# The first MLP by seven products of quarters, with its squares through DRAM and the state-space matrices written beside its down half

## The chip, the cores and the metric

One core of one Trainium2 chip runs the whole program. The metric is the device time of one execution in microseconds. The core's engines work side by side, each through its own list of instructions in order: TensorE (PE, with the weight loads PEld beside it), VectorE (DVE), ScalarE (ACT) and GpSimd (POOL). SyncE (SP) issues nearly all DMAs from one queue, in order as well.

## The reference

Two layers on x of 1024 tokens by 1024 channels, all in float32:

```python
for i in range(2):
    u = rms_norm(h, norm_mix[i])
    h = h + (diff_attention(u, ...) if i == 0 else s5_layer(u, ...))
    h = h + square(relu(rms_norm(h, norm_ffn[i]) @ w_up[i])) @ w_down[i]
```

`w_up[i]` is 1024 by 4096 and `w_down[i]` 4096 by 1024. The S5 layer (a state-space layer: a complex diagonal recurrence in both directions over 64 groups of 16 channels, then a gated projection) depends on its parameters through matrices that can be made at any time before it: input and output matrices, rotations and short convolution kernels for every group.

## The kernel before

Activations lie transposed: a tile of 128 channels by 1024 tokens, eight of them in `hT`. A float32 product is made of three: operand and weight are each split into a rounded high part (ACT) and the remainder (DVE), and high x high, low x high and high x low are summed in PSUM (`mm3`, L202). So 128 x 1024 outputs over 1024 channels take 8 x 3 x 2 = 48 matmuls of 512 columns. Weights come through `WStream` in tiles of 512 KB: three raw buffers, ACT makes `whi` (L66), DVE makes `wlo` (L67).

**The stages** in order: q, k and v projections; attention; the output projection `wo` (`psw`); the first MLP; the S5 layer with its gated projection; the second MLP; the transposed write of the output.

**The first MLP** (`run_mlp`) goes in eight blocks of four hidden tiles. `up(f)` makes a hidden tile with 48 matmuls (`psu`), DVE applies relu and the norm (`mz`, L649), ACT squares, ACT and DVE split the square into `sh` and `sl`, which stay in SBUF. `down(b)` multiplies a block's four tiles into all eight tiles of the output (`psd`, 24 matmuls each) and DVE adds each to `hT` (L667). Over the MLP that is 1536 matmuls up and 1536 down.

**The second MLP** has another scheme already. Input and weights of two hidden tiles (a pair, 16 in all) are cut in quarters, and seven products of sums of quarters stand for eight (Strassen's way): a pair takes 7 x 12 = 84 matmuls (`psX`, `psY`, `psQ`, L986) in place of 96. DVE and ACT make the sums and splits of the next pair's weights meanwhile (`w_sums_a`, `w_sums_b`, `w_group_a`, `w_group_b`, L844 to L879), DVE adds up the products and applies relu (`finish`, L996), and the squares go to DRAM (`sD`) and are read back (`sr`) for the down half, which runs in four blocks of eight hidden tiles, 48 matmuls for each of 32 steps. This part stands in a manual schedule: its instructions keep the order in which they are written. Everything else is ordered by the framework's scheduler, which works by a simulated timeline: it hoists an instruction to where it believes that its engine would be free.

**The state-space matrices** are made by `Prep`: `start` computes powers and angles (161 small instructions on DVE), and `tile(kt)`, eight times, makes the matrices of eight groups. A tile's work: products of 128 elements on POOL (B, C), then in four quarters the matrix W (six complex-product instructions of 256 elements on DVE, L1295 to L1297), PE transposes, ACT copies, `INd` to DRAM; the matrix Y (six instructions of 256 elements on POOL, one buffer `Yt`), `Yd` to DRAM; small matmuls (`ppk`); and the rotations R (42 DVE instructions in seven doubling levels, one buffer `Rt`, L1295 to L1297), `Rd` to DRAM. At the end the kernel matrix goes to `Kd`. In this kernel `start` stands ahead of the first MLP and `tile(b)` ahead of `down(b)`. The S5 layer reads all of it back, and starts with transposes of `hT` (`pu`) and, after `pin` and a copy, its scans on DVE (L1506 is the first instruction of one).

Of the kernel before, what the change touches and what calls it, by code (L numbers as in the profile page):

```python
# [104 lines left out]
def _build(ctx, tc, nc, a, out):  # L105
# [41 lines left out]
    def mlp_src(i):  # L147
        r = []
        for b in range(9):
            ups = [(kt_cols(wup[i], f * P, P), (8, P)) for f in range(4 * b, 4 * b + 4)] if b < 8 else []  # L150
            dns = (
                [
                    (wdn[i][(b - 1) * 512 : b * 512, q * 256 : (q + 1) * 256].rearrange("(k p) n -> p k n", p=P), (4, 256))
                    for q in range(4)
                ]
                if b
                else []
            )
            r += ups[:1] + dns + ups[1:]
        return r  # L160
# [22 lines left out]
    for f in range(32):  # L183
        src.append((kt_cols(wup[1], f * P, P), (8, P)))
    for b in range(4):
        for m in range(KT):
            src.append((wdn[1][b * 1024 : (b + 1) * 1024, m * P : (m + 1) * P].rearrange("(k p) n -> p k n", p=P), (8, P)))
# [345 lines left out]
    hT = hv.tile([P, KT, S], F32, name="hT", tag="hv")  # L533
    prep = Prep(const, tc, nc, a, dram, ident)
    ctx.callback(prep.close)
    mlp = phase.enter_context(tc.tile_pool(name="mlp", bufs=2, reuse_waits="tile"))
    psm = phase.enter_context(tc.tile_pool(name="psm", bufs=2, space=PSUM, reuse_waits="tile"))
    turn = [0]

    def acc_tile(name):  # L540

        if psl is None:
            return psm.tile([P, S], F32, name=name, tag="ps")
        turn[0] += 1
        if turn[0] % 3:
            return psm.tile([P, S], F32, name=name, tag="ps")
        return [psl.tile([P, 512], F32, name=name, tag="b") for _ in range(2)]

    def pieces(ps):

        if isinstance(ps, list):
            return [(slice(512 * t, 512 * t + 512), ps[t]) for t in range(2)]
        return [(slice(0, S), ps)]

    def bank(ps, t):
        return ps[t] if isinstance(ps, list) else ps[:, 512 * t : 512 * t + 512]

    class Norm:
# [16 lines left out]
        def done(self):  # L575
# [5 lines left out]
            for c, b in pieces(ps):  # L581
                nc.scalar.activation(self.acc[:, c], b, AF.Ln, bias=eps_t, scale=1.0 / D)
# [196 lines left out]

    xs = {}
# [833 lines left out]
```

## Time and profile before

| what | value |
|---|---|
| median of 3 runs | 2500.45 us (2498.51 to 2503.64) |
| the profiled execution | 2497.23 us, its span 2495.3 us |
| granted TensorE clock, mean | 0.994 |
| busy: PE / DVE / ACT / POOL | 97% / 66% / 41% / 12% |
| chain that ended last | PE 71%, DVE 18%, ACT 3%, DMA 3%, issue 3% |

Busy shares are means over stages of quite different kinds. The chain of waits is followed back from the last instruction, at each step to what released it. Matmuls follow each other at a shorter distance than the duration shown for one, since they are pipelined: the distance is read from the chain, where a piece has a count and a length. In the stretches of the view by windows, busy time counts overlapping instructions once.

### The profile page before, as it was taken

The page shows a single profiled execution, that of the slowest core. Times are in us where ns is not written, and L with a number is a line of the kernel's source. Part 1 is how long each engine was busy: PE and PEld are TensorE (multiplying, and loading weights), DVE is VectorE, ACT ScalarE, POOL GpSimd, SP SyncE. Part 2 cuts the span into 40 slices and gives each one's busy share as a digit, 9 for nine tenths or more (in the row PEclk, how much of TensorE's full clock was granted, in tenths as well). Part 3 has the DMA queues.
Part 4 walks back from the last instruction along what each step waited for, and adds up shares of the span by engine and source line. Part 5 has one row for each costly group of instructions (what it writes and reads, how often), then busy time and mean ns, then how long its engine had stood idle before and what let it go on. Part 6 is the DMA issues. An engine that isn't in the chain of part 4 may idle for free.

```text
span 2495.3 us, 33696 instructions
## 1 busy us (share of the span) xinstructions
PE 2409.3 (97%) x12338; PEld 2031.0 (81%) x12338; DVE 1635.3 (66%) x3473; ACT 1019.1 (41%) x1808; POOL 299.6 (12%) x452
## 2 busy tenths in 40 slices
PE   7999999999998999999999997999999999999999
PEld 6889988888787778778788886787878888788887
DVE  5765188888468898888873457994876666432321
ACT  5654277777242212222122137883454333321111
POOL 1221000000004242242241230000000000000000
PEclk9999999999999999999999998999999999999999
DMA  6666524231212232322232236552223334632322
GB/s 158 187 182 181 118 64 102 56 97 43 61 43 77 82 95 78 95 86 84 87 94 65 70 136 184 171 164 76 85 70 112 103 110 135 198 110 68 101 59 60
DMA packets 295173, 258.78 MB, mean 104 GB/s; under 512 B 43232, under 2 KB 266080, under 8 KB 295008
## 3 DMA queue, kind: packets, MB, share of 16 engines
q1 hardware_dynamic: 289120, 248.00, 33.9%
q10 hardware_dynamic: 5888, 8.63, 1.3%
q8 instruction: 97, 1.59, 0.3%
q14 instruction: 68, 0.56, 0.1%
HBM read 180.09 MB, written 68.09 MB: 99 GB/s over the span
## 4 chain that ended last, share of the span: by engine, by line
PE 71%; DVE 18%; ACT 3%; DMA 3%; issue 3%; SPq 1%; POOL 0%; ACTq 0%; DVEq 0%; POOLq 0%
PE psd L202 22%; PE psu L202 9%; PE psq L202 7%; PE psX L986 6%; PE psw L202 4%; PE pss L425 3%; PE po L475 3%; PE psh L216 3%; PE psQ L986 3%; DVE tr L1296 2%; DVE Rt L1297 2%; PE pT L462 2%; PE psg L202 2%; DVE wlo L67 1%; DVE mx L432 1%
## 5 line engine op out<-in xcount | busy, mean ns | idle before, releaser
L66 ACT ACTIVATE whi<-wraw 128x1024 fp32r<-128x1024 f32 (+1 forms) x145 | 152.7, 1054 | 618.3 <-PE psd L202 298.3
L202 PE MATMUL psd<-sh,wlo 128*128 128x512 f32 x1024 | 329.1, 397 | 0.0
L202 PE MATMUL psd<-sh,whi 128*128 128x512 f32 x1024 | 324.7, 395 | 0.0
L202 PE MATMUL psd<-sl,whi 128*128 128x512 f32 x1024 | 323.3, 394 | 0.0
L67 DVE TENSOR_TENSOR wlo<-wraw,whi 128x1024 fp32r<-128x1024 f32 (+1 forms) x145 | 178.7, 1233 | 86.7 <-ACT whi L66 86.6
L202 PEld LDWEIGHTS psd<-sl,whi 128*128 128x128 f32 x1024 | 191.0, 188 | 40.2
L202 PEld LDWEIGHTS psd<-sh,wlo 128*128 128x128 f32 x1024 | 191.2, 188 | 39.7
L202 PEld LDWEIGHTS psd<-sh,whi 128*128 128x128 f32 x1024 | 190.2, 188 | 38.5
L1127 DVE TENSOR_TENSOR hT<-hT,psd 128x512 f32<-128x512 f32 x64 | 41.2, 684 | 206.0 <-PE psd L202 206.0
L432 DVE TENSOR_REDUCE mx<-pss 128x1 f32<-128x1024 f32 x128 | 155.4, 1221 | 13.8 <-PE pss L425 13.8
L440 ACT ACTIVATE e<-pss,mx 128x1024 f32<-128x1024 f32 x128 | 142.9, 1116 | 52.2 <-DVE mx L432 49.6
L202 PE MATMUL psu<-ah_u,whi 128*128 128x512 f32 x512 | 159.5, 392 | 0.0
L202 PE MATMUL psu<-ah_u,wlo 128*128 128x512 f32 x512 | 158.6, 391 | 0.0
L202 PE MATMUL psu<-al_u,whi 128*128 128x512 f32 x512 | 158.4, 391 | 0.0
L475 PEld LDWEIGHTS po<-V,pt 128*128 128x128 f32 x1024 | 128.0, 191 | 5.5
L475 PE MATMUL po<-V,pt 128*128 128x128 f32 x1024 | 132.4, 275 | 0.0
L202 PEld LDWEIGHTS psu<-ah_u,whi 128*128 128x128 f32 x512 | 95.6, 188 | 21.0 <-issue 0.7
L202 PEld LDWEIGHTS psu<-al_u,whi 128*128 128x128 f32 x512 | 95.7, 188 | 19.7
L202 PEld LDWEIGHTS psu<-ah_u,wlo 128*128 128x128 f32 x512 | 95.7, 188 | 19.6
L845 DVE TENSOR_TENSOR wlo<-wraw,whi 128x1024 fp32r<-128x1024 f32 x48 | 58.8, 1226 | 75.9 <-ACT whi L844 75.9
L667 DVE TENSOR_TENSOR hT<-hT,psd 128x512 f32<-128x512 f32 (+1 forms) x88 | 80.3, 922 | 40.6 <-PE psd L202 40.6
L1297 DVE TENSOR_TENSOR Rt<-Rt,tr 128x2 f32<-128x2 f32 (+6 forms) x448 | 102.2, 228 | 6.3
(401 smaller groups left out, 5342.6 us busy)
## 6 DMA issues: line engine op xcount, KB each, us to landing
wraw<-in_ffn_w_up_dram SPq DMA_DIRECT2D x64, 512.0 KB, 4.4
wraw<-in_ffn_w_down_dram SPq DMA_DIRECT2D x64, 512.0 KB, 3.7
sr<-sD SPq DMA_DIRECT2D x32, 512.0 KB, 4.3
wraw<-in_attn_w_qkv_dram SPq DMA_DIRECT2D x24, 512.0 KB, 4.8
sD<-s SPq DMA_DIRECT2D x48, 256.0 KB, 2.2
xt<-in_x_dram SPq DMA_DIRECT2D x16, 512.0 KB, 5.8
zs<-z ACTq DMA_DIRECT2D x64, 128.0 KB, 4.4
q<-qs SPq DMA_DIRECT2D x16, 512.0 KB, 6.7
```

Of the source, the lines that this page charges most:

```text
L66: self.nc.scalar.activation(hi, t, AF.Copy)
L67: self.nc.vector.tensor_tensor(lo, t, f32(hi), op=ALU.subtract)
L202: nc.tensor.matmul(ps[t] if isinstance(ps, list) else ps[:, c], wt[:, k, n0 : n0 + P], x[k][:, c], start=k == 0 and i == 0, stop=k == nk - ...
L216: nc.tensor.matmul(ps, wt[:, kk, n0 : n0 + P], x[k][:, c], start=start and kk == 0 and i == 0, stop=stop and kk == last and i == 2)
L425: nc.tensor.matmul(ps[:, c], q[:, qt * P : (qt + 1) * P], k[:, c], start=i == 0, stop=i == 1)
L432: nc.vector.tensor_reduce(mx, w["ps"][m], axis=AX.X, op=ALU.min)
L440: nc.scalar.activation(e, w["ps"][m], AF.Exp, bias=w["mx"][m], scale=-1.0, accum_out=s)
L475: nc.tensor.matmul(w["po"], w["pt"][:, k, :], V[:, k, h * P : (h + 1) * P], start=k == 0, stop=k == KT - 1)
L667: nc.vector.tensor_tensor(hT[:, m, c], hT[:, m, c], p, op=ALU.add)
L845: nc.vector.tensor_tensor(lo, raw, f32(hi), op=ALU.subtract)
L986: nc.tensor.matmul(ps, wt[:, j, kk, :], xx, start=start and kk == 0 and i == 0, stop=kk == 3 and i == 2, skip_group_check=not start)
L1297: E.tensor_tensor(o, o, tmp, op=op)
```

## The change

The scheme of the second MLP becomes a function, `fast_up(lay, tail, ...)`, with the down half in `down(u, on_step, on_last)`, and the first MLP uses both. `TailO` gives what runs at the head of the manual schedule: in layer 0 the last three tiles of the output projection, as the last two of the gated projection in layer 1. The first MLP's PSUM tiles are six banks of 512 in place of eight, since two are kept for `Prep`. SBUF has no room for all of it at once, so `hT` goes to DRAM (`hA`) tile by tile, comes back into another tile, `hTb`, once the operands B11 and R1 are used up, and its old place becomes the memory of `Prep` (`prepmem`, cut up by `Carve`). After the down half `hT` is read back once more (`hTc`) into the place of `prepmem`. `Prep.start` is written behind the up half, and `tile` once in four steps of the down half, the eighth behind the last step. R is made for four groups at a time, in half as many instructions of twice the size.

```diff
     def mlp_src(i):
-        r = []
-        for b in range(9):
...
+        r = [(kt_cols(wup[i], f * P, P), (8, P)) for f in range(32)]
+        for b in range(4):
+            for m in range(KT):
+                r.append((wdn[i][b * 1024 : (b + 1) * 1024, m * P : (m + 1) * P].rearrange("(k p) n -> p k n", p=P), (8, P)))
         return r
...
+    def fast_up(lay, tail, gp, xpool, wx, gw, nacc, open_banks, free_ops, first_f):
...
-    def run_mlp(i, hi, lo, on_last, on_block):
...
+    def down(u, on_step, on_last):
+        bank1, hid, nf, ring = u["bank1"], u["hid"], u["nf"], u["ring"]
+        while nf < 8:
+            u["split"](nf)
+            nf += 1
+        for b in range(4):
+            for m in range(KT):
+                w = ws.next()
...
+                    mm3(ps, w, 0, ([y[0] for y in x], [y[1] for y in x]), halves=halves)
+                for t in range(2):
+                    c = slice(512 * t, 512 * t + 512)
+                    nc.vector.tensor_tensor(hT[:, m, c], hT[:, m, c], ps[t], op=ALU.add)
...
+                on_step(b, m)
+                if b == 3:
+                    on_last(m)
...
+    st = phase.enter_context(tc.tile_pool(name="st0", bufs=6, space=PSUM, reuse_waits="tile"))
+    psl = phase.enter_context(tc.tile_pool(name="psl0", bufs=2, space=PSUM, reuse_waits="tile"))
...
+        nc.sync.dma_start(h0[m], hT[:, m, :])
...
+    up0 = fast_up(0, TailO(), gp, {"B11": xpa, "R1": xpa, "B21": xpb}, wx, gw, nacc, banks0, ("B11", "R1"), 1)
+    xpa_stack.close()
+    hT = pool("hB").tile([P, KT, S], F32, name="hTb")
+    for m in range(KT):
+        nc.sync.dma_start(hT[:, m, :], h0[m])
+    prep = Prep(const, tc, nc, a, dram, ident, hv.tile([P, KT * S], F32, name="prepmem", tag="hv"))
+    prep.start(psl)
...
+    down(up0, lambda b, m: prep.tile(2 * b + m // 4) if m % 4 == 3 else None, last0)
...
+    hT = hv.tile([P, KT, S], F32, name="hTc", tag="hv")
+    for m in range(KT):
+        nc.sync.dma_start(hT[:, m, :], hD[m])
...
-            R = t("Rt", (2, 2, P))
+            if hf % 2 == 0:
+                continue
+            q4 = slice(g0 + 2 * hf - 2, g0 + 2 * hf + 2)
+            R = t("Rt", (4, 2, P))
```

**DVE in the up half of the first MLP.** Before, between two hidden tiles (`mz` is a hidden tile's relu, `Rt` and `tr` the rotations):

```order
L1297 TENSOR_TENSOR Rt<-Rt,tr 128x2x32
L1296 TENSOR_TENSOR tr<-Rt,sn 128x128
L649 SCALAR_TENSOR_TENSOR mz<-psu,nacc 128x512
L1297 TENSOR_TENSOR Rt<-Rt,tr 128x2x64
L649 SCALAR_TENSOR_TENSOR mz<-psu,nacc 128x512
L67 TENSOR_TENSOR wlo<-wraw,whi 128x1024
L1296 TENSOR_TENSOR tr<-Rt,cs 128x128
```

In the changed kernel, in the fourth pair (`wraw` lines are the next pair's sums of quarters, `s_7425` a sum of products, `prepmem` is what `Prep` makes: 128x4 and 128x4x2 are levels of R, 128x8x2x16 parts of W):

```order
L621 SCALAR_TENSOR_TENSOR wraw<-wraw 128x512
L1350 TENSOR_TENSOR prepmem<-prepmem 128x4
L622 TENSOR_TENSOR wraw<-wraw 128x512
L1349 TENSOR_TENSOR prepmem<-prepmem 128x4
L1348 TENSOR_TENSOR prepmem<-prepmem 128x4x2 x2
L795 TENSOR_TENSOR s_7425<-s_7425,psX 128x512
L1348 TENSOR_TENSOR prepmem<-prepmem 128x8x2x16 x2
L1350 TENSOR_TENSOR prepmem<-prepmem 128x4
L722 SCALAR_TENSOR_TENSOR s_7425<-s_7425,nacc_6121 128x512
L1350 TENSOR_TENSOR prepmem<-prepmem 128x8x2x16
L1349 TENSOR_TENSOR prepmem<-prepmem 128x4x2
```

The scheduler has moved the work of `Prep` from where it is written, behind the up half, into the up half: between the first pair's products and the first addition of the down half DVE has 864 of its instructions (163 of `start`, 571 of R, 115 of W, 15 others), and 194 stand beside the down half (133 of R, 55 of W, 6 others); 25 follow it.

**SP between the up and the down half.** `sr` are the squares that come back for the down half (the first step takes the hidden tiles 0 to 7), `hTb` waits for the last use of R1, in the sixteenth pair:

```order
L739 DMA sr<-sD_2_6889 128x1024
L1001 DMA hTb<-hA_6143 128x1024
L1001 DMA hTb<-hA_6144 128x1024
L1001 DMA hTb<-hA_6145 128x1024
L1001 DMA hTb<-hA_6146 128x1024
L739 DMA sr<-sD_3_6890 128x1024
L1001 DMA hTb<-hA_6147 128x1024
L1001 DMA hTb<-hA_6148 128x1024
L1001 DMA hTb<-hA_6149 128x1024
L1001 DMA hTb<-hA_6150 128x1024
L739 DMA sr<-sD_4_6891 128x1024
```

Before, no such load stood between the first MLP's halves, and its squares did not go through DRAM.

**PE at the end of the first MLP.** Before (`psd` down half, `pp` and `kk` the last of the eighth tile of `Prep`, `psr` the norm of the tokens, `pu` the first of the S5 layer):

```order
L202 MATMUL psd<-sh,wlo 128x512 x2
L1415 MATMUL pp_14024<-ident,kk 128x128
L1415 MATMUL pp_14027<-ident,kk 128x128
L590 MATMUL psr<-ones,nacc 128x1 x8
L1439 MATMUL pu<-ident,hT 128x128 x8
```

In the changed kernel (`ppc` opens a tile of `Prep` on PE):

```order
L190 MATMUL psd<-sh,wlo 128x512
L889 MATMUL psr<-ones,nacc_9325 128x1
L1430 MATMUL pp_12809<-ident,prepmem 128x128
```

and from the last `psr` on:

```order
L889 MATMUL psr<-ones,nacc_9325 128x1 x4
L1473 MATMUL pp_12877<-ident,prepmem 128x128
L1473 MATMUL pp_12880<-ident,prepmem 128x128
L1374 MATMUL ppc<-ident,prepmem 128x128 x2
L1392 MATMUL pp_13173<-prepmem 128x128
L1393 MATMUL pp_13173<-prepmem 128x128
L1430 MATMUL pp_13190<-ident,prepmem 128x128 x2
```

The eighth tile of `Prep` has moved from beside the down half to behind it: all of its rows on PE, from `ppc` on, stand between the last `psd` and `pu<-ident,hTc`, which comes 17 rows below the last one shown. On POOL the two clears of the S5 layer's `X` now stand ahead of that tile's C and Y products, and on SP the eight loads of `hTc` stand behind its last store.

## Rows read from the trace of the kernel before

**Rows 1.** The page's busy times: us, share of the span, instructions.
```profile
PE 2409.3 (97%) x12338; PEld 2031.0 (81%) x12338; DVE 1635.3 (66%) x3473; ACT 1019.1 (41%) x1808; POOL 299.6 (12%) x452
```

**Rows 2.** Windows: stretch, length, busy us (instructions) of PE, PEld, DVE, ACT, POOL; clock.
```profile
722.00:1500.00 778.00, 761.65 (x3524) 621.99 (x3522) 592.58 (x2037) 191.41 (x345) 228.93 (x354) 1.00 0.28 86
1811.00:1865.00 54.00, 47.85 (x197) 37.55 (x196) 41.22 (x59) 29.42 (x45) 0.00 (x0) 0.97 0.18 59
1865.00:2126.00 261.00, 258.96 (x1142) 213.76 (x1141) 157.93 (x202) 103.44 (x152) 0.00 (x0) 1.00 0.39 120
2139.00:2418.00 279.00, 279.00 (x1237) 231.19 (x1236) 95.84 (x106) 56.72 (x56) 0.00 (x0) 1.00 0.32 98
```

**Rows 3.** The chain of waits in order of time: start us, length us, what, count.
```profile
721.59 9.74 PE psu L202 x42
...
1320.39 32.66 PE psu L202 x144
...
1403.94 10.93 PE psd L202 x47
...
1493.72 4.27 PE psd L202 x18
...
1772.63 38.09 PE psg L202 x168
...
2139.55 277.45 PE psd L202 x1224
```

**Rows 4.** Windows of L1295, L1296, L1297 alone: DVE, then POOL, busy us (instructions).
```profile
722.00:1500.00 778.00, 105.36 (x512) 68.56 (x96) 1.00 0.28 86
722.00:1500.00 778.00, 136.68 (x512) 59.98 (x96) 1.00 0.28 86
722.00:1500.00 778.00, 130.85 (x512) 70.93 (x96) 1.00 0.28 86
```

**Rows 5.** Tile Rt and line L1296: duration ns min/median/max; then waits of Rt's engine.
```profile
L1297 DVE TENSOR_TENSOR Rt<-Rt,tr x448: 146/176/822, 769.6 to 1286.6; 128x2 f32<-128x2 f32 x22, 128x16 f32<-128x16 f32 x22, 128x128 f32<-128x128 f32 x22, 128x4 f32<-128x4 f32 x21
L1296 DVE TENSOR_TENSOR tv<-pi,Bi x32: 408/424/851, 779.0 to 1473.9; 128x256 f32<-128x256 f32 x32
  DMA Rd<-Rt: 44.0, 19
```

**Rows 6.** Groups by line and shape: busy us, mean ns, idle before and releaser.
```profile
L1297 DVE TENSOR_TENSOR W<-W,tv 128x256 f32<-128x256 f32 x64 | 31.6, 493 | 2.5 <-issue 2.2
L1297 POOL TENSOR_TENSOR Yt<-Yt,tw 128x256 f32<-128x256 f32 x64 | 55.8, 871 | 2.1
L1295 POOL TENSOR_TENSOR Yt<-pr,Car 128x256 f32<-128x256 f32 x32 | 25.7, 804 | 57.2 <-PE ppk L1392 56.4 <-DMA Yd<-Yt 0.7
L1295 POOL TENSOR_TENSOR Yt<-pr,Can 128x256 f32<-128x256 f32 x32 | 23.5, 735 | 0.0
L1296 POOL TENSOR_TENSOR tw<-pi,Car 128x256 f32<-128x256 f32 x32 | 22.6, 707 | 2.1
L1295 POOL TENSOR_TENSOR Car<-cssm_c_re,ar 128x128 f32<-128x128 f32 x8 | 7.3, 913 | 305.8 <-ACT cssm_c_re L1323 305.8
L1296 POOL TENSOR_TENSOR tmp<-cssm_c_im,ai 128x128 f32<-128x128 f32 x8 | 3.3, 413 | 32.3 <-ACT cssm_c_im L1323 32.3
L1429 POOL MEMSET X<- 128x512 f32 x2 | 1.0, 526 | 9.2 <-PE psd L202 9.2
```

**Rows 7.** Timeline at the start of the S5 layer: start us, length us, what, idle before.
```profile
1504.53 1.95 PE L1439 MATMUL pu<-ident,hT 128*128 128x128 f32 x8
1514.67 0.69 DVE L1506 TENSOR_TENSOR A<-s,R 128x512 f32<-128x512 f32 x1 [4.13 <-DMA T<-Kd]
```

**Rows 8.** DMA issues: what, queue, count, KB each, median us from issue to landing.
```profile
Yd<-Yt SPq DMA_DIRECT2D x32, 256.0 KB, 2.3
hT<-hD SPq DMA_DIRECT2D x2, 512.0 KB, 4.3
Kd<-full SPq DMA_DIRECT2D x8, 120.0 KB, 3.8
```

More of the change, by code (lines that the diff above doesn't have):

```diff
@@ L972, in _build @@
-    gps.close()
-    st = phase.enter_context(tc.tile_pool(name="st", bufs=8, space=PSUM, reuse_waits="tile"))
-    sD = [dram.tile([P, S], F32, name=f"sD{f}") for f in range(32)]
-    def bank1(name):
-        return st.tile([P, 512], F32, name=name, tag="st")
-    def product(ps, w, j, op, start=True):
-        for kk in range(4):
-            x = x_of(op, kk)
-            for i, (wt, xx) in enumerate(((w[0], x[0]), (w[0], x[1]), (w[1], x[0]))):
-                nc.tensor.matmul(
-                    ps, wt[:, j, kk, :], xx, start=start and kk == 0 and i == 0, stop=kk == 3 and i == 2, skip_group_check=not start
-                )
@@ new lines, in _build, with start, nrm, mm6 @@
+    class TailG:
+        def start(self, x_left):
+            x_left(0)
+            x_left(1)
+            self.pss = {}
+        def nrm(self, m, t):
+            TailO.nrm(self, m, t)
+        def mm6(self, half):
+            w = ws.next()
+            self.pss[6, half] = psm.tile([P, S], F32, name="psg2", tag="ps")
+            mm3(self.pss[6, half], w, 0, (yhi, ylo))
+        def first(self):
+            self.mm6(0)
+        def second(self):
+            self.mm6(1)
+        def weights(self):
+            self.w7 = [ws.next(), ws.next_ready()]
+        def half0(self):
+            pss = self.pss
+            for half in range(2):
+                if half:
+                    pss[7, half] = [psg.tile([P, 512], F32, name="psg2", tag="psg") for _ in range(2)]
+                else:
+                    pss[7, half] = psm.tile([P, S], F32, name="psg2", tag="ps")
+                mm3(pss[7, half], self.w7[half], 0, (yhi, ylo), halves=(0,))
+                if half == 0:
@@ new lines, in half0, with half1, rest, end @@
+                        gated(6, t, pss[6, 0][:, c], pss[6, 1][:, c])
+                        self.nrm(6, t)
+        def half1(self):
+            mm3(self.pss[7, 0], self.w7[0], 0, (yhi, ylo), halves=(1,))
+            gated(7, 0, self.pss[7, 0][:, 0:512], self.pss[7, 1][0])
+        def rest(self):
+            mm3(self.pss[7, 1], self.w7[1], 0, (yhi, ylo), halves=(1,))
+        def end(self):
+            gated(7, 1, self.pss[7, 0][:, 512:1024], self.pss[7, 1][1])
+    def banks1():
+        gps.close()
+        st = phase.enter_context(tc.tile_pool(name="st", bufs=8, space=PSUM, reuse_waits="tile"))
+        bank1 = lambda name: st.tile([P, 512], F32, name=name, tag="st")
+        return bank1, lambda: [bank1("psn") for _ in range(2)]
```

822 lines of the change are left out of this document (399 added, 423 removed).

## The prediction, made before the run

> **What bounds the kernel now.** The page's busy times come first: PE is busy for 97% of the span [rows 1]. That is a mean, so the next view is the windows by stage. The first MLP, from 722 to 1500 us, has PE busy for 761.65 of 778 us, and DVE for 592.58 [rows 2]: PE is the bound there, with 16.4 us of idle time, and DVE has a quarter of its time free. In the steady pairs of the second MLP, 1865 to 2126, PE has 258.96 of 261 us and DVE 157.93. The chain of waits gives PE's pace, since its pieces have counts: `psu` 32.66 us for 144 matmuls, 0.2268 each; `psd` of the first MLP 10.93 for 47, 0.2326; `psd` of the second 277.45 for 1224, 0.2267 [rows 3]. The reader should see that the two MLPs already stand side by side in one trace, so most terms of this change have a row of their own.
>
> The first MLP begins at 721.6 us and its last `psd` ends at 1493.72 + 4.27 = 1498.0 [rows 3]: 776.4 us. Its 3072 matmuls are 1536 x 0.2268 + 1536 x 0.2326 = 705.6 us. Of the 778 us of its window 72.4 remain; less 16.4 of idle that is 56 us of PE for the eight tiles of state-space matrices, small matmuls and the slower ones behind them: 7 us a tile.
>
> **The change part by part.** *Seven products.* 16 pairs x 84 = 1344 matmuls replace 1536: 192 x 0.2268 = 43.5 us less on PE. A pair is 84 x 0.2267 = 19.04 us.
>
> *The start of the scheme.* The gated projection ends at 1772.63 + 38.09 = 1810.7 [rows 3], and the second MLP's first two pairs end at about 1865: 54 us, with PE busy for 47.85 [rows 2]. Two steady pairs are 38.1, so the first pair costs 54 - 19 = 35 us, with the splits of its input. `TailO` does the same at the end of the output projection, and I take 35 for the first pair there too.
>
> *The other 15 pairs: PE or DVE.* PE needs 15 x 19.04 = 285.6 us, and 4.2 tiles of `Prep` stand in the up half in PE's order: 29 us, together 315. DVE needs, for the pairs alone, 157.93 us in 261 / 19.04 = 13.7 pairs [rows 2], 11.5 a pair, 173 in all. Beside it now stand 864 instructions of `Prep`. Their price is the question of this change. The three lines of complex products took 105.36 + 136.68 + 130.85 = 372.9 us for 1536 instructions on DVE [rows 4]: 0.243 each. The 686 of R and W in the up half are 167 us at that, the 178 others at 0.2, between the shortest rows and that mean, 36 us. **DVE needs 173 + 203 = 376 us where PE needs 315**, and DVE is the bound of the up half. Low end: R and the others at their shortest, 0.146, W at 0.41 [rows 5]: 749 x 0.146 + 115 x 0.41 = 156, in all 329. High end: the new R runs over levels of 4 to 256 elements in place of 2 to 128, which puts an instruction near 0.493 [rows 6] in place of one near 0.176 [rows 5], a seventh of 0.32 more on each: 686 x 0.288 + 178 x 0.24 = 240, in all 413. I take 376, from the mean, since it holds the waits of one product for another within a chain, which the new chains have too. That R has one buffer and DVE waited 44.0 us for its stores in 19 cases [rows 5] I count at nothing: the sets lie further apart now.
>
> The Trainium skill ("Perfetto Trace Analysis", section Optimizing Scalar/DVE Operations) states otherwise: about 60 ns of overhead per DVE instruction, and a reported latency of about twice that, whose second half overlaps with the next instruction. By it the short products would cost about half of what they show, and DVE would just keep up, which is the first rival below. The trace agrees only in part, with 0.243 us a product [rows 4].
>
> *The seam to the down half.* The first step takes eight hidden tiles read back from DRAM, and on SP four loads of `hTb` stand ahead of the fourth square and four more ahead of the fifth. A load of 512 KB lands after 4.3 us [rows 8]; thirteen loads, two in flight at a time, are 28 us, and two weight tiles 4 more. PE has three products and most of a step ahead of it, 18 us. The stall is at most 14 to 20 us, and nothing if DVE's delay has made PE late anyway. I take 8.
>
> *The down half.* 1536 x 0.2267 = 348 us, at the pace of the same code in the second MLP [rows 3] (357 at the old pace of 0.2326), and 2.8 tiles of `Prep`, 20 us: 368. DVE has 194 instructions of `Prep` here and in the second MLP's down half was busy for 95.84 of 279 us [rows 2]: no bound.
>
> *The end of the MLP.* Today 1514.67 - 1498.0 = 16.7 us pass from the last `psd` to the S5 layer's first scan [rows 3, 7]. In the changed kernel the eighth tile of matrices stands whole behind the last `psd`. Its POOL part waits behind the clearing of `X`, which waited for the last `psd` already in this trace [rows 6]. Then C: seven instructions of 0.41 to 0.91, 4 us; Y: four times 0.804 + 0.735 + 2 x 0.707 + 2 x 0.871 = 4.7 us [rows 6], 18.8; one buffer, so three waits for a landing of 2.3 [rows 8], 7 at most; the rest of the seventh tile, about 3; the copies and transposes of the last matrix 1.5, its store 3.8, and only then, since `hTc` takes the place of `prepmem`, a load of 4.3 [rows 8]. From `pu` to the scan it is 10.1 us [rows 7] with 4.13 of wait for loads that come earlier now: 6 to 7. The sum is 49; against 16.7 today **32 us more**. Low end 15, if POOL's waits overlap with it and the rows of POOL, which are rough, read long; high end 45, if small loads queue behind the eight of 512 KB.
>
> The stores of `hA`, the squares' stores and the two PSUM banks fewer I cost at nothing: with DVE as the bound PE has time to wait for a bank or a weight tile. Were PE the bound, a pair would lose at most the wait for one product, 12 x 0.2267 = 2.7 us.
>
> **Sum.** 35 + 376 + 8 + 368 = 787 against 776.4: 11 us more; with 32 at the end 43 us more. 2497.2 + 43 = 2540 on the profiled execution's own time; the median stands 3 us above it, so **2543 us**.
>
> **The rivals.** *DVE keeps up.* Independent products overlap: DVE needs 329, hidden waits are few and PE's 315 decide, at about 325. Then 35 + 325 + 4 + 368 = 732, 44 us less, and with 22 at the end 22 less: **2478 us**. It decides wherever DVE's price of a short product is below (315 - 173 - 115 x 0.41) / 749 = 0.127 us. For it: in today's window DVE does its work at 76% busy and PE hardly waits. Against it: 0.243 a product, and its shortest rows at 0.146 are above that point.
>
> *Every queue late.* DVE at 413, the seam at 20 and the end at 45: 35 + 413 + 20 + 368 = 836, 60 more, with 45 at the end 105 more: **about 2605 us**. For it: four engines that run in order and wait for each other lose more than the busiest of them needs.
>
> *The change does not do what it says.* The matrices are not made beside the down half, as the order shows. If the scheduler's hoisting hurt nothing and only the end stayed, gain and loss would cancel: 2497 to 2505.
>
> **How the numbers follow.** My forecast, DVE the bound at about its mean price and an exposed end, gets 0.60 and reaches from 2510 to 2580, all slower. DVE keeping up gets 0.24, nearly all faster. Every queue late gets 0.11, slower. The cancelling case gets 0.05. A measurement of this kernel tells about 0.2%, 5 us, from no change. So faster 0.22, same 0.06, slower 0.72. The range from 2474 to 2592 takes in the keeping-up case and leaves out the worst of the late one; the forecast's own range is 2510 to 2580.
>
> **What would show it.** Right: in the up half of the first MLP DVE is busy for over 90% and PE for about 85%, pairs last 23 to 26 us in place of 19, PE's idle time there ends at DVE; in the down half `psd` runs at 0.227; between the last `psd` and the first scan lie about 49 us, in which POOL makes Y and PE stands. Wrong: pairs of 20 us with DVE at 85%, or `pu` within 25 us of the last `psd`. A long stall ahead of the first `psd` would show the seam mis-sized.

## The result, and the profile after

The changed kernel takes 2567.2 us (median of 4 runs, 2563.39 to 2568.27) against 2499.5 of the kernel before beside it (2496.19 to 2503.64): a ratio of 1.0267, 95% interval 1.0248 to 1.0286. It is 68 us slower. Forecast were 2543 us, 43 us slower, in a range of 2474 to 2592. Its profiled execution took 2563.39 us, with a span of 2561.7.

First the page of the changed kernel: busy times, then DVE and the granted TensorE clock in 40 slices of 64 us (tenths).

```profile
PE 2393.4 (93%) x12146; PEld 2016.5 (79%) x12146; DVE 1649.0 (64%) x2903; ACT 1075.4 (42%) x1881; POOL 324.9 (13%) x452
...
DVE  5764288886479999989533555996776666532321
...
PEclk9999999999988999999999996999999999999999
```

PE works 16 us less than before [rows 1], in a span that is 66 us longer. Slices 13 to 19 of DVE's row (six of 9 and one of 8) are most of the up half of the first MLP and the first steps of its down half. The two slices of 8 and the one of 6 in PEclk are its early pairs and the end of the MLP. The windows by stage (columns as in [rows 2], then DMA share and GB/s) say the same in numbers.

```profile
722.00:1142.00 420.00, 354.36 (x1543) 284.75 (x1543) 384.64 (x1063) 151.61 (x264) 146.95 (x196) 0.93 0.41 123
1142.00:1190.00 48.00, 44.15 (x196) 35.30 (x195) 44.18 (x92) 17.60 (x26) 25.49 (x32) 0.93 0.87 289
1190.00:1520.00 330.00, 330.00 (x1506) 273.48 (x1506) 156.04 (x308) 70.84 (x95) 52.98 (x84) 1.00 0.37 113
1520.00:1580.00 60.00, 32.31 (x153) 25.80 (x152) 22.38 (x43) 17.66 (x48) 30.70 (x48) 0.60 0.57 193
```

In the up half DVE is busy for 92% and PE for 84%, in the rest of the down half PE for 100%, and behind it for 54%. The waits of PE from 720 to 1142 us (what it waited for, us, times, longest):

```profile
PE psX L712 <- ACT s L761: 34.4, 14, 7.9
PE psX L712 <- ACT whi L587: 12.1, 1, 12.1
PE psX L712 <- ACT s L779: 8.5, 6, 3.8
PE psX L712 <- DVE s L795: 5.5, 4, 1.7
```

ACT stands in these rows but is busy for 36% of this stretch. The copy `s` at L761 reads the bank that the next `psX` needs, and ACT runs it behind the square of L723, for which it waits for DVE's relu at L722. The first two rows of ACT's own waits in the same stretch:

```profile
ACT s L723 <- DVE s L722: 131.9, 38, 13.1
ACT mz L723 <- DVE mz L722: 27.6, 11, 4.4
```

That relu stands in DVE's queue among products of `Prep`. So products of 0.2 us each, which nobody needs yet, delay PE by way of DVE and ACT.

The end of the MLP is in the chain of waits (start us, length us, what):

```profile
1529.59 1.28 ACT L891
1531.92 2.09 DMA prepmem<-in_ssm_c_im_dram
...
1542.79 2.19 DMA Yd<-prepmem
...
1549.09 2.35 DMA Yd<-prepmem
...
1555.67 2.16 DMA Yd<-prepmem
...
1564.23 1.68 DMA Kd<-prepmem
1566.17 3.56 DMA hTc<-hD
1569.77 1.98 PE pu L1497 x8
...
1580.70 0.69 DVE A L1564
```

From 1531.92 on that is the eighth tile: its C, Y through one buffer with three waits for a landing, the last matrix, and only then the load of `hTc`.

By the starts of instructions in the trace, the difference of 66 us in the span divides like this. The output projection ends 3 us earlier. The MLP, from there to its last `psd`, takes 807 us in place of 777: 43 for the first pair with its head, 393 for the other 15 pairs, 371 for the down half. Then 54 us in place of 17 pass until the first scan. The S5 layer up to its `psh` takes 2 us more, and from there to the end nothing changes (798.7 us, 799.1 before).

### The profile page after: what moved, and what is told of

Same layout as the page of the kernel before. It is cut to its first block, busy times and chain, and to the rows that moved or that the text cites. A ratio compares the mean times of both kernels' runs of the same rounds, so it can differ in the third digit from the quotient of the medians.

```text
span 2561.7 us, 33013 instructions
## 1 busy us (share of the span) xinstructions
PE 2393.4 (93%) x12146; PEld 2016.5 (79%) x12146; DVE 1649.0 (64%) x2903; ACT 1075.4 (42%) x1881; POOL 324.9 (13%) x452
## 4 chain that ended last, share of the span: by engine, by line
PE 70%; DVE 17%; ACT 5%; DMA 3%; issue 3%; POOL 2%; SPq 0%; ACTq 0%; POOLq 0%; DVEq 0%
PE psd L190 25%; PE psX L712 9%; PE psq L190 7%; PE psQ L712 5%; PE pss L413 3%; PE po L463 3%; PE psh L204 3%; PE psw L190 3%; PE psY L712 2%; PE psg L190 1%; PE pT L450 1%; DVE mx L420 1%; PE psv L373 1%; PE psv L372 1%; DVE wlo L588 1%
## 5 line engine op out<-in xcount | busy, mean ns | idle before, releaser
L588 DVE TENSOR_TENSOR wlo<-wraw,whi 128x1024 fp32r<-128x1024 f32 x96 | 118.8, 1238 | 90.8 <-ACT whi L587 90.7
L856 DVE TENSOR_TENSOR hTc<-hTc,psd 128x512 f32<-128x512 f32 x64 | 41.2, 684 | 205.4 <-PE psd L190 205.4
L723 ACT ACTIVATE s<-s 128x512 f32<-128x512 f32 x96 | 60.6, 632 | 264.4 <-DVE s L722 262.3
L712 PE MATMUL psX<-xhi_T,whi 128*128 128x512 f32 x256 | 110.8, 433 | 49.9 <-ACT s L761 34.4
L748 DVE TENSOR_TENSOR sl<-sr,sh 128x1024 fp32r<-128x1024 f32 x64 | 79.4, 1242 | 81.3 <-ACT sh L747 80.3
L856 DVE TENSOR_TENSOR hTb<-hTb,psd 128x512 f32<-128x512 f32 x64 | 41.4, 683 | 115.2 <-PE psd L190 115.2
L587 ACT ACTIVATE whi<-wraw 128x1024 fp32r<-128x1024 f32 x96 | 100.3, 1045 | 27.1 <-DVE wraw L622 15.8
L747 ACT ACTIVATE sh<-sr 128x1024 fp32r<-128x1024 f32 x64 | 67.8, 1060 | 98.5 <-DMA sr<-sD 92.1
L712 PE MATMUL psX<-xhi_T,wlo 128*128 128x512 f32 x256 | 106.2, 415 | 0.0
L1348 POOL TENSOR_TENSOR prepmem<-prepmem 128x256 f32<-128x256 f32 (+1 forms) x96 | 76.0, 805 | 237.9 <-ACT prepmem L1376 128.1
```

Source lines behind the costliest of these rows:

```text
L587: nc.scalar.activation(hi, raw, AF.Copy)
L588: nc.vector.tensor_tensor(lo, raw, f32(hi), op=ALU.subtract)
L712: nc.tensor.matmul(ps, wt[:, j, kk, :], xx, start=start and kk == 0 and i == 0, stop=kk == 3 and i == 2, skip_group_check=not start)
L748: nc.vector.tensor_tensor(sl, sr, f32(sh), op=ALU.subtract)
L856: nc.vector.tensor_tensor(hT[:, m, c], hT[:, m, c], ps[t], op=ALU.add)
```

## Experiments

Two theories stood against each other for the pairs. DVE: `Prep`'s instructions, which the scheduler hoists into the up half, fill VectorE, and the pairs wait for it. PIPE: six PSUM banks in place of eight, the squares' way through DRAM or the lower clock slow the pairs, and DVE's load only fills the waits. For the end: TILE (the eighth tile) against RELOAD (the loads of `hTc`). The table holds all runs. The three stretches are worked out from starts in each trace: pairs 2 to 16; from the last `psX` to the last `psd`; from the start of the last `psd` to the first scan. The ratio is that to the kernel before, with its interval. The text counts the pairs from 1; the expectations count from 0, so that their pair 2 is the third.

| kernel | us | ratio | 15 pairs | down half | to the scan |
|---|---|---|---|---|---|
| before | 2499.5 | | | | 16.8 |
| changed | 2567.2 | 1.0267 (1.0248 to 1.0286) | 392.9 | 370.5 | 54.7 |
| e1_short_r | 2537.0 | 1.0137 (1.0120 to 1.0154) | 359.2 | 372.7 | 56.5 |
| e3_tiles_early | 2545.4 | 1.0179 (1.0163 to 1.0196) | 391.1 | 380.1 | 21.6 |
| e7_late_r | 2541.6 | 1.0160 (1.0145 to 1.0175) | 345.1 | 385.2 | 58.7 |
| e8_late_r_early | 2526.3 | 1.0100 (1.0085 to 1.0115) | 345.4 | 403.6 | 24.6 |
| e2_swap | 2558.8 | 1.0233 (1.0217 to 1.0248) | 291.7 | 437.9 | 79.8 |
| e14_no_y | 2524.8 | 1.0102 (1.0083 to 1.0121) | 358.2 | 368.6 | 47.3 |
| e9_merged_r | 2508.2 | 1.0037 (1.0023 to 1.0051) | 344.3 | 383.8 | 25.1 |
| e10_pool_powers | 2517.5 | 1.0068 (1.0053 to 1.0083) | 351.2 | 386.4 | 26.4 |
| e11_first_pair | 2530.9 | 1.0124 (1.0109 to 1.0139) | 350.1 | 387.9 | 23.2 |
| e12_copies | 2499.7 | 0.9999 (0.9990 to 1.0008) | 344.7 | 385.1 | 19.7 |
| e13_short_powers | 2499.2 | 0.9998 (0.9988 to 1.0008) | 348.3 | 383.3 | 18.1 |

### Fewer products in the up half

```diff
-            for lv in range(7):
+            for lv in range(1):
```

> The changed kernel, with the loop that builds the rotations R cut from seven levels to one (the rest of R is set by memset; its values are not computed, so that part of the computation is left out). Nothing else moves but the instructions that the scheduler had put beside R. Theory DVE (mine): the pairs of the up half last 26.2 us because VectorE has the state-space matrices beside them. About 490 of the 571 short products leave the up half, at 0.2 to 0.243 us each 98 to 119 us of DVE; its 385 us of 420 fall to some 270 to 285, below PE's 315. Then the 15 pairs take 310 to 330 us in place of 393 (20.5 to 22 each), the steps 0 to 2 of the down half lose the 10 to 18 us that they had over 10.9 each, the time falls to 2470 to 2505 us, and the granted clock of the up half rises from 0.93 towards 0.99. Theory PIPE (rival): six PSUM banks, the squares' way through DRAM or the lower granted clock slow the pairs, and VectorE's load only fills the waits. Then pairs stay at 25 to 26 us and the time is 2545 us or more.

The pairs lost 34 us, not 63 to 83, and the time 30. PIPE had given them nothing, so it is hurt, but the size was missed, and the down half did not fall at all (372.7 against 370.5). DVE's busy time in the pairs fell from 361 to 287 us, 80% of their 359, and PE still waits: pairs 3 to 6 keep 25 to 32 us, since there the powers of `start` and the first tiles' W stand in DVE's queue, and PE waits for it although it is not full.

### R held back

```diff
+    prep.rp = wx
...
-            R = t("Rt", (4, 2, P))
+            R = self.rp.tile([P, 1024], F32, name="Rt", tag="wxhi").rearrange("p (g i n) -> p g i n", g=4, i=2)
...
-            tr = t("tr", (4, 64))
+            tr = self.rp.tile([P, 1024], F32, name="tr", tag="wxlo")[:, 0:256].rearrange("p (g n) -> p g n", g=4)
```

> The changed kernel, with all products kept, but the two buffers of R's making in a pool whose tiles the pairs use until the end of the up half, so that R can't be hoisted into it: DVE's instructions of the state-space matrices there fall from 838 to 339, and some 190 to 240 stand in each of the first three blocks of the down half. Theory DVE: pairs fall to 20 to 22 us, 15 of them to 300 to 330 in place of 393; the down half takes VectorE 75 to 90 us a block where PE needs 87 and its share of the tiles, so it grows by at most 0 to 25 us; the end stays (54 us). Time 2490 to 2520 us. Theory PIPE: pairs stay at 25 us or more, time 2555 to 2590.

The 15 pairs fell by 48 us to 345, short of 300 to 330, and the down half grew by 15, within its 0 to 25. The time, 2541.6, missed its 2490 to 2520: the pairs gave less, and the wait behind the last `psd` grew by 4. The window of the pairs shows DVE below PE now, and the clock back:

```profile
763.00:1108.00 345.00, 322.55 (x1498) 264.46 (x1498) 270.90 (x514) 137.15 (x238) 140.87 (x189) 0.99 0.45 137
```

Some pairs are down to 20.0 us with the same six banks and the same traffic. What stays long are pairs 3 and 4, 32.1 and 25.6 us: there DVE runs the powers of `start`, a chain in which each power waits for the one ahead.

### The pairs without any of it

```diff
-    hT = pool("hB").tile([P, KT, S], F32, name="hTb")
+    hT = hv.tile([P, KT, S], F32, name="hTb", tag="hv")
...
-    prep = Prep(const, tc, nc, a, dram, ident, hv.tile([P, KT * S], F32, name="prepmem", tag="hv"))
+    prep = Prep(const, tc, nc, a, dram, ident, pool("hB").tile([P, KT * S], F32, name="prepmem"))
...
-    hT = hv.tile([P, KT, S], F32, name="hTc", tag="hv")
-    for m in range(KT):
-        nc.sync.dma_start(hT[:, m, :], hD[m])
```

> The changed kernel with two homes swapped: hTb comes into the old place of hT, so that no reload is needed, and the memory of the state-space matrices lies where the operands B11 and R1 were, which are in use until the sixteenth pair. So neither the matrices nor the powers ahead of them (start) can be made beside the pairs: in the up half VectorE has the pairs alone but for the last one. The runs before left 17 us of PE's waits in pairs 2 and 3, in which VectorE runs the powers, 250 ns a step, and about 20 us for the rest of the pairs' excess, which is small matmuls on PE. Theory DVE: pairs 2 to 14 take 19.0 to 19.6 us each, 15 pairs 288 to 300 (392.9 in the changed kernel), with the same six banks, the same squares through DRAM. Theory PIPE: 22 us or more each. The matrices then stand in the down half, 200 to 250 instructions of VectorE a block, and about two tiles behind the last psd: the down half grows by 25 to 50 us and the wait behind it by 10 to 30. Time 2510 to 2550 us.

This settles PIPE. Pairs 4 to 15 take 19.0 us each, and the window over 14 of them is the second MLP's of the kernel before again (258.96 of 261 us and 157.93 of DVE, [rows 2]):

```profile
783.00:1049.00 266.00, 266.00 (x1173) 219.78 (x1172) 163.13 (x214) 105.89 (x155) 1.00 (x5) 1.00 0.40 122
```

Six banks, squares through DRAM at 122 GB/s: none of it costs PE anything. Of the 101 us that the pairs gave 92 came back all the same: 67 us in the down half, where DVE now has 384 us of work in 438, and 25 behind it, where two tiles wait for POOL (`ppk` for 29.0 us in 15 waits). The time missed its range by 9 us, since the down half grew by more than the 50 that I had given it.

```profile
1054.00:1492.00 438.00, 404.32 (x1857) 327.26 (x1856) 384.08 (x1157) 100.69 (x174) 191.34 (x277) 0.96 0.44 136
1492.00:1580.00 88.00, 44.91 (x197) 35.14 (x195) 39.30 (x72) 23.87 (x67) 47.44 (x77) 0.57 0.35 107
```

### The end of the MLP

```diff
-    down(up0, lambda b, m: prep.tile(2 * b + m // 4) if m % 4 == 3 else None, last0)
+    down(up0, lambda b, m: prep.tile((8 * b + m) // 3) if (8 * b + m) % 3 == 2 and 8 * b + m < 24 else None, last0)
```

> The changed kernel, with the eight tiles of state-space matrices written at steps 2, 5, ..., 23 of the down half's 32 in place of steps 3, 7, ..., 31, so that none stands behind the last psd; the reload of hTc still waits for the last use of prepmem. Theory TILE (mine): the 45 us between the last psd and pu are the eighth tile, of which the reload of 4.3 us is the smallest part. Then pu comes 8 to 14 us behind the last psd, the first scan 17 to 22 us behind it (54.3 in the changed kernel), pairs stay at 26 us, and the time falls by 30 to 37 us to 2530 to 2537. Theory RELOAD (rival): the wait is for the eight loads into the old place, queued behind other loads. Then it falls by less than 10 us, to 2557 or more.

TILE holds: `pu` comes 4.9 us behind the last `psd`, the first scan 21.6, and the pairs are what they were. But only 22 us were gained, not 30 to 37: the tile's work stands in the down half now, 10 us longer, and the scan has a wait of its own. The chain of this run:

```profile
1535.68 0.70 DVE hTb L856
1536.39 9.74 DMA hD<-hTb
1546.20 3.64 DMA hTc<-hD
1549.86 0.41 SPq L1520
1550.32 2.77 DMA IN<-INd
...
1560.81 0.69 DVE A L1564
```

The last tile goes to DRAM and back (9.74 and 3.64 us), and the first load of the S5 layer stands behind it on SP. RELOAD was the smaller part, and it shows once the tile is gone.

The two edits together:

> Both: R held out of the up half as in the run before, and the tiles at every third step as in the one before that. If both theories (DVE for the pairs, TILE for the end) hold, the two gains are in different stretches and add: pairs of 20 to 22 us and the first scan 17 to 22 us behind the last psd, time 2455 to 2490 us, below the kernel before (2499). If VectorE becomes the bound of the down half, with a tile every third step (56 to 66 us of the matrices in a block and 31 of its own, beside 87 of PE's psd and 20 of PE for the tiles), the down half grows by 20 to 40 us and the time is 2490 to 2520. If PIPE holds, 2530 or more.

Apart the edits gave 25.6 and 21.8 us, together 40.9. The down half is 33 us longer than in the changed kernel, which is the second of the three cases, 6 us above its range: three steps take 17.0, 18.3 and 19.3 us. In the first two DVE is busy for 14.3 of 17 and 17.5 of 18 us, with products of R among its own work. In the third it is busy for 11.1 of the 20 us around it; there PE stands behind a transpose of `Prep` (`pp`) that waits 3.7 us for an ACT copy, which itself waits for stores of `INd` to land.

### What makes a product dear

The price of a product was the prediction's main estimate. Two places of DVE's timeline in the changed kernel (start us, length us, what):

```profile
840.26 0.16 DVE L1348 TENSOR_TENSOR prepmem<-prepmem 128x4 f32<-128x4 f32 x1
840.33 0.15 DVE L1349 TENSOR_TENSOR prepmem<-prepmem 128x4 f32<-128x4 f32 x1
840.40 0.16 DVE L1348 TENSOR_TENSOR prepmem<-prepmem 128x4 f32<-128x4 f32 x1
...
844.64 0.95 DVE L1349 TENSOR_TENSOR prepmem<-prepmem 128x8 f32<-128x8 f32 x2
845.52 0.94 DVE L1350 TENSOR_TENSOR prepmem<-prepmem 128x8 f32<-128x8 f32 x2
```

and POOL's timeline at that time:

```profile
838.13 0.70 POOL L1349 TENSOR_TENSOR prepmem<-prepmem 128x256 f32<-128x256 f32 x1
843.67 2.44 POOL L1348 TENSOR_TENSOR prepmem<-prepmem 128x256 f32<-128x256 f32 x2 [4.84 <-PE ppk L1445]
846.07 1.00 POOL L1350 TENSOR_TENSOR prepmem<-prepmem 128x256 f32<-128x256 f32 x1
```

With POOL idle, products of 4 elements follow each other every 0.07 us. With POOL running, two products of 8 elements take 0.95; where POOL stands, one of 8 takes 0.163 (30 cases in the 15 pairs). That is a coincidence until POOL is taken away:

```diff
-            for i, (x, y) in enumerate(((Car, Cai), (Can, Car))):
-                cmul(Y[:, :, i].rearrange("p g j h -> p j g h"), (fwd(prr), bb(x)), (fwd(pii), bb(y)), ALU.subtract, tg)
+            E.memset(Y, 0.0)
```

> The changed kernel, with GpSimd's twelve products of a quarter tile's Y replaced by one memset (Y's values are not computed, so that part of the computation is left out); VectorE's instructions and their order stay what they are (700 products of the matrices in the up half in place of 699). In the trace of the changed kernel a product of 128x4 elements on VectorE takes 0.16 us where GpSimd stands and 0.38 on the mean where it runs, a 64x64 one 0.22 and 0.37, while additions from PSUM take 0.68 in both. If GpSimd's reading is what makes VectorE's products dear (theory PORT), the 607 products of the 15 pairs fall from 0.31 us to 0.22 to 0.26 each, 30 to 50 us less of VectorE, and the 15 pairs from 393 to 350 to 375 us. If the two only happen at the same time (loads, waits within a chain), the products stay above 0.29 and the pairs above 383. Either way the wait behind the last psd loses Y's chain there, some 25 us.

PORT holds. The groups of products in DVE's order, 761 to 1154 us, first the changed kernel, then this run (busy us, mean ns, idle before):

```profile
L1350 DVE TENSOR_TENSOR prepmem<-prepmem 128x256 f32<-128x256 f32 (+6 forms) x202 | 65.8, 333 | 1.4
L1349 DVE TENSOR_TENSOR prepmem<-prepmem 128x256 f32<-128x256 f32 (+6 forms) x203 | 65.1, 327 | 4.2 <-POOL prepmem L1350 1.4 <-DVE prepmem L1350 0.3
L1348 DVE TENSOR_TENSOR prepmem<-prepmem 128x256 f32<-128x256 f32 (+6 forms) x202 | 57.9, 321 | 1.2 <-PE pp L1430 1.0
```

```profile
L1349 DVE TENSOR_TENSOR prepmem<-prepmem 128x256 f32<-128x256 f32 (+6 forms) x221 | 59.8, 278 | 3.8 <-POOL prepmem L1350 0.9
L1350 DVE TENSOR_TENSOR prepmem<-prepmem 128x256 f32<-128x256 f32 (+6 forms) x220 | 59.7, 279 | 1.5
...
L1348 DVE TENSOR_TENSOR prepmem<-prepmem 128x256 f32<-128x256 f32 (+6 forms) x222 | 51.9, 269 | 1.2 <-PE pp L1430 1.0
```

By busy time that is 188.8 / 607 = 0.311 us a product with Y on POOL, and 171.4 / 663 = 0.259 without. (This run's stretch takes in the first steps of its down half; its 15 pairs alone give 0.260.) Shape by shape, where POOL stands a product costs the same in both runs, 0.162 us for 128x4 and 0.163 for 128x8; over all cases in the 15 pairs it falls from 0.260 to 0.190 and from 0.282 to 0.165. So it is not another mix of shapes. The pairs fell by 35 us to 358, inside 350 to 375, and the time by 42. DVE is busy for 326.5 of 356 us there, 92% as before, with 34 us less to do, while PE's own waits for POOL in the pairs had been 3.2 us. So POOL's six products of a quarter tile (the twelve of the expectation are a slip), which cost POOL nothing that matters, cost PE about 35 us, by these numbers nearly all of it by way of DVE.

The wait behind the last `psd` lost 7 us, not 25. The chain of this run shows why: without Y, ACT's copies of W, which go to DRAM through one buffer, are the next chain in line, with five waits for landings of `INd` (12.4 us in all).

The Trainium skill ("SBUF — State Buffer", section Who interferes with whom) states that a DVE instruction with two SBUF inputs contends with a GpSimd instruction that reads SBUF; these runs agree, and so do the additions from PSUM, which have one SBUF input and take 0.68 us whether POOL runs or stands.

### On to a better version

The first step keeps R late and the tiles early, and makes R by three products of twice the size a level:

```diff
-                c0, s0 = R[:, :, 0, 0:n], R[:, :, 1, 0:n]
-                cmul(R[:, :, 0, n : 2 * n], (c0, wr), (s0, wi), ALU.subtract, tr[:, :, 0:n], nc.vector)
-                cmul(R[:, :, 1, n : 2 * n], (c0, wi), (s0, wr), ALU.add, tr[:, :, 0:n], nc.vector)
+                cmul(R[:, :, :, n : 2 * n], (R[:, :, :, 0:n], wr), (R[:, :, ::-1, 0:n], wi), ALU.add, tr[:, :, :, 0:n], nc.vector)
```

> The run with R late and tiles early (2526 us), with R made by half as many instructions: the real and the imaginary part of a level in one (cos, sin) tile, three products of twice the size in place of six, with a signed copy of the sines. 336 products of 8 to 512 elements stand for 672 of 4 to 256. If VectorE's time for R is what stretches the down half there (steps of 17.0, 18.3 and 19.3 us, 403.6 in all against 370.5), it falls by 12 to 25 us, and the time to 2500 to 2515 us. If the steps are long by PE's small matmuls alone, the time stays at 2520 to 2530.

The down half lost 20 us and the time came to 2508, both as expected, and DVE's busy time in the down half fell from 305 to 266 us:

```profile
1108.00:1492.00 384.00, 376.59 (x1749) 309.65 (x1748) 265.74 (x590) 91.44 (x141) 115.28 (x165) 0.99 0.47 146
```

Next, the powers on GpSimd:

```diff
-                    V.tensor_tensor(o[s, e[i], :], pr[s, e[i - 1], :], x[s], op=ALU.mult)
+                    nc.gpsimd.tensor_tensor(o[s, e[i], :], pr[s, e[i - 1], :], x[s], op=ALU.mult)
```

> The run before, with the 84 dependent instructions of the powers (pr, pi) moved from VectorE to GpSimd, which is idle in the first pairs. If VectorE's chain of powers makes the waits of pairs 2 and 3 (11.5 and 5.4 us beyond PE's own work), they fall by 8 to 14 us, and the time to 2488 to 2505 us. If GpSimd's instructions hold VectorE up where both run, the pairs around 785 to 850 us get longer instead, and the time does not fall.

The second case came, 9 us slower than the run before: on POOL a power's instruction takes 418 to 472 ns, B and C of the first tile stand behind them, and PE waits for them in a small matmul with `psX` queued behind it. Two rows of PE's waits from 780 to 850 us:

```profile
PE psX L712 <- DVE s L795: 7.4, 2, 5.8
PE pp L1396 <- POOL prepmem L1354: 6.6, 1, 6.6
```

Then the head of the first pair in another order:

```diff
         ws._load()
         ws._load()
+        ta, tb = ws.loaded[0][0], ws.loaded[1][0]
+        rawp[0] = [ta, tb]
+        Wg[0] = {1: group(ta, ws.sp, "whi", "wlo")}
         tail.half0()
...
         tail.rest()
+        w_sums_b(0)
+        w_group_b(0)
+        w_sums_a(0)
```

> The run before, with another order in the head of the first pair: the splits of the first group of weights come ahead of the last tile of the output projection, and the weight sums, which only the third product needs, behind the splits of the last input tile. PE waits 12.1 us for these splits between psw and psX in the changed kernel. If it is the order on VectorE that makes it wait, psX starts 2 to 4 us behind psw and the waits move in part into the first pair (which has 10.4 us of its own): 5 to 10 us less, 2480 to 2500 us. If the first pair is bound by VectorE's sum of work up to its fourth product, the time stays within 3 us.

A miss. `psX` starts 0.2 us behind `psw` in place of 12.5, but the pair then takes 42.5 us in place of 30.7, so both together take what they took. DVE is busy for 35.8 of these 42.3 us (36.7 of 42.8 in the changed kernel): here the amount of its work counts, not the order, though no run takes work out of the head to show it. Since both MLPs use the function, the second one's head changed too, and from its last `psg` to its second pair it takes 41.8 us in place of 28.0, which is the 13 us that the whole lost: there the order does count. That the edit reached both MLPs was not in my expectation.

From the run with the merged R again, `hTc` by copies:

```diff
-        nc.sync.dma_start(hT[:, m, :], hD[m])
+        if m % 2:
+            nc.vector.tensor_copy(hT[:, m, :], hb[:, m, :])
+        else:
+            nc.scalar.activation(hT[:, m, :], hb[:, m, :], AF.Copy)
```

> The run with the merged R (2508 us), with hTc filled by eight copies from hTb on ScalarE and VectorE in place of eight loads of 512 KB from hD (hD is still stored, since it is read later). There 25 us pass from the last psd to the first scan, 16.7 in the kernel before: pu waits 4.2 us for hTc, and then the first scan 10.6 us, of which PE waits 8.6 for loads of IN that stand behind the eight loads on SP. If the loads are what is late, the first scan comes 15 to 19 us behind the last psd, and the time falls by 6 to 10 us to 2498 to 2502. If the state-space loads are late by themselves (the matrices are stored late), it falls by 0 to 4 us.

The scan comes 19.7 us behind the last `psd`, a little outside 15 to 19, and the time is 8.5 us less, as expected: 2499.7, level with the kernel before. Of the 8.5 us, 5.4 lie between the last `psd` and the scan; in the profiled executions 2.3 more lie ahead of the first pair, where nothing was changed. Last, on top of it, the powers by doubling:

```diff
-            for i in range(1, 8):
-                for o, x, y, op in ((pr, ar, ai, ALU.subtract), (pi, ai, ar, ALU.add)):
+        for n in (2, 4):
+            V.tensor_tensor(sr, br, br, op=ALU.mult)
...
+            for o, x, y, op in ((pr, sr, si, ALU.subtract), (pi, si, sr, ALU.add)):
```

> The run before this one, with the powers made by doubling, on VectorE: 38 instructions of 64 to 256 elements in place of 84 dependent ones of 64. The waits beyond PE's own work in pairs 2 and 3 (13.2 and 2.7 us with the merged R) are VectorE's chain of powers at about 250 ns a step: 46 steps fewer are 11 us less of VectorE, less 3 for the wider ones. If VectorE is what they wait for, they fall by 6 to 10 us, and the time to 2488 to 2496 us, 0.2 to 0.5% below the kernel before. If the other engines' order makes that wait, as in the run with the powers on GpSimd, it stays within 3 us of the run before this one.

No gain. Pair 3 takes 34.7 us, 33.6 before. The windows of that stretch, first with the long powers, then with the short ones:

```profile
785.00:819.00 34.00, 25.11 (x93) 19.55 (x92) 32.39 (x104) 10.54 (x17) 11.25 (x20) 0.85 0.32 84
```

```profile
787.00:822.00 35.00, 24.13 (x93) 19.22 (x92) 34.32 (x86) 10.75 (x17) 16.98 (x28) 0.85 0.32 81
```

DVE is as full, with 86 instructions in place of 104: the place of the powers was taken by W's products of the first tile, which the scheduler hoisted further, with POOL busier beside them. No version beat the kernel before; the best two are within 0.1% of it.

## Why the prediction was right, and where it was not

*Sign and mechanism.* Right: DVE became the bound of the up half, PE's idle time there ends at what DVE is late with, and the eighth tile stands exposed behind the last `psd`. The measured 68 us against 43 forecast lie inside the range. Term by term, the first pair took 8 us more than forecast, the other pairs 17 more, the seam and the down half 5 less, the end 6 more; outside these, 3 us less passed ahead of the MLP and 2 more behind the scan. The pairs took 26.2 us on the mean, just over the 23 to 26 that were to show it. The mechanism has a limit: e1_short_r and e14_no_y have pairs of the same length (359 and 358 us) with DVE busy for 80% and 92%. So the pairs do not follow DVE's busy time alone; that it matters when the relus get their turn in its queue is my reading of the waits.

*The matmuls saved (43.5 us).* Right: 84 a pair at 19.04 us is what e2_swap's pairs show to the tenth. The gain is real, and it is spent elsewhere.

*The first pair (35 us).* It took 43. The row I took it from was the wrong one to copy, and I read it wrong: 1810.7 is the end of one piece of the chain, the last `psg` starts at 1815.8, and from there the second MLP's first pair with its head takes 28 us. So the 35 had 7 us to spare, and the first MLP took 15 more than that row. There PE waits 12.1 us for the split of the first weights, ahead of which DVE has the sums of three input tiles; DVE itself had stood 4.84 us for the last weights of the output projection, whose load is in the chain with 4.72. e11_first_pair shows that another order of that work gains nothing.

*The other 15 pairs (376 us, of which the forecast had PE 315).* They took 393. The window of these pairs:

```profile
761.00:1154.00 393.00, 340.98 (x1508) 276.08 (x1507) 360.54 (x1008) 139.22 (x243) 155.21 (x203) 0.94 0.44 137
```

DVE's total was near: busy for 360.5 us, where I had 376 of work. That is in part luck. The price of a product by my measure was too low, 0.311 in place of 0.243; it didn't raise the sum, since that measure adds the three lines' busy times, which overlap (188.8 us by line, 172 together), and fewer of them ran in these pairs (607 products) than I had put there (686). The step that failed is that an engine with 376 us of work finishes in 376 us: DVE stood for 32 us, 13.6 of them for ACT's `whi`. The rival that said that engines in order wait for each other, "every queue late", priced the pairs at 413.

*What the 107 us over 15 x 19.04 are.* Worked out from the starts of matmuls: 29 are `Prep`'s small matmuls, as forecast; 52 are PE's waits; and 21 are matmuls that step at more than 0.3 us, mostly 0.43, on a lower clock, which had no term in my sum. Of the 5 that are left, 4 are 17 `psd` of the down half that stand ahead of the last `psX`.

*POOL beside DVE.* It had no term either. The price that I took from the kernel before contained it already, since POOL ran for 229 of 778 us there [rows 2], and I read the mean as waits within a chain: a product of 128x4 took 0.161 us there where POOL stood (114 cases) and 0.338 where it ran for over half of it (67). In the changed kernel POOL runs for 155 of the 393 us of the 15 pairs, and the price rose. The range of 0.146 to 0.493 that I gave held both.

*The Trainium skill's 60 ns* ("Perfetto Trace Analysis", section Optimizing Scalar/DVE Operations), which carried the rival "DVE keeps up": the trace agrees for independent products with POOL idle, 0.07 us apart at 840.26. It doesn't hold for the sum, by POOL and by the dependent products (the powers step at 0.25 us). The rival fell.

*The seam (8 us) and the down half (368 us).* Together 376, measured 371 from the last `psX`, 374 with the 17 `psd` ahead of it. The pace was 0.227 as predicted: steps 4 to 19 take 10.9 us each, and the chain has them, from the third step on, in one piece:

```profile
1185.12 195.75 PE psd L190 x856
```

The first three steps took 51 us: 33 for their `psd`, 5 for the last 24 `psX`, which stand in the first one, 5 for `Prep`'s small matmuls, and 8 in which PE waited or stepped slower. So the seam came out at the 8 that I took; since that was a pick between nothing and 20, the hit is luck. The chain has loads of `hTb` ahead of the squares there and DVE's last hoisted work beside the splits. The tiles' small matmuls took 15 us in place of 20, and 3 went to slower steps later on.

*The end (49 us, 32 more than before).* It took 54, 38 more. C and Y took 28 us in place of 30, the last matrix 2.8 in place of 1.5, its store and the reload 5.5 in place of 8. Too short were the way from the last `psd` to C, 8.4 us in place of 3 (in it a small load, 2.09 in the chain, that was left out), and the way from `pu` to the scan, 9.4 in place of 6 to 7.

*"Not the way the change says".* The order had shown that the matrices stand beside the up half, and the prediction used it. That was the step on which the sign hung.

Open is how much of the end's lower clock (0.60 in that window) adds to it; no run separates it.

## What to carry to other kernels

Work off the critical path that a scheduler hoists into a stretch is free only while every engine that it uses stays below the stretch's bound: compare its instructions with that engine's slack there, stage by stage, and hold it back by where its memory comes free if it does not fit. Taking some of it away need not help, since other work moves up into the gap: look at the engine's busy share after the edit, not at what was taken out. And a saving on the bound is worth what the next engine leaves in that stage, not on the mean: seven products for eight gave PE 43 us, and DVE's total hardly grew (607 us from 722 to 1580, where the MLP before had 593 from 722 to 1500), but it was busy for 92% of the up half and for 47% of most of the down half.

## What the runs showed of the hardware that I had not expected

VectorE's products of two SBUF tiles are slowed by GpSimd's, and the short ones the most. Over 761 to 1154 us of the changed kernel, a product of 128x4 takes 0.162 us on the mean where POOL stands (34 cases) and 0.364 where it runs for over half of it (35 cases); one of 128x256, 0.42 and 0.58; additions from PSUM 0.68 in both.

In this trace a wait of PE cost more than its length. Between 815 and 856 us of the changed kernel PE waited twice for a bank, 7.9 and 3.06 us, the second time up to 855.60. Then it ran six matmuls at 0.23 us a step, eight at 0.43, and the next at 0.23 again. The windows (the sixth number behind the stretch's length, counts left out, is the granted clock):

```profile
847.00:855.60 8.60, 5.54 (x28) 4.39 (x26) 8.39 (x29) 2.75 (x5) 3.84 (x4) 1.00 0.45 137
855.60:857.10 1.50, 1.50 (x6) 1.23 (x7) 1.50 (x5) 0.22 (x1) 0.00 (x0) 0.98 1.19 306
857.10:860.10 3.00, 3.00 (x8) 2.32 (x7) 2.59 (x9) 1.16 (x3) 0.00 (x0) 0.50 0.32 114
860.50:862.80 2.30, 2.30 (x11) 1.88 (x10) 1.98 (x4) 1.30 (x3) 0.00 (x0) 1.00 0.34 125
```

So the granted clock fell to the lower of its two levels (0.50, 1.2 GHz) in a stretch in which PE had no gap, after one in which it had waited, and came back. Over the 15 pairs such steps make 21 us, beside 52 us of waits. With 27 us of waits they make 10 in e14_no_y and 15 in e1_short_r, with 22 they make 7 in e7_late_r, and in e2_swap, whose pairs wait for 1 us in all, under 1.
